# Split weights kept as one tile whose start moves by 8 bytes from use to use

## The chip, the cores and the metric

The kernel runs on one NeuronCore of a Trainium2 chip. The metric is device time in microseconds, from the start of the program on that core to its end. Each time given for a kernel is a median of runs; the profile is one further execution of the same program. The engines are called PE (the matrix engine), DVE (the vector engine), ACT (the scalar engine), POOL and SP; of SP only the queue is used, it issues most of the transfers.

## What is computed

A token block of 256 rows and 1024 columns passes two transformer blocks in float32. The first has two layers, and each layer works on the rows (`lat`) and on a context of 256 rows (`cx`) together; the second has memory attention, dilated attention, a convolution branch and a mixture of 32 experts.

```python
for l in range(DEPTH):                       # first block, two layers
    lat = lat + 0.5 * ml[2] * _swiglu(_modulate(lat, ...), *ffn1)
    cx = cx + 0.5 * mc[2] * _swiglu(_modulate(cx, ...), *ffn1)
    out_lat, _, _ = _token_mixer(_modulate(lat, ...), *mix_w, s_f, s_b)
    lat = lat + ml[5] * out_lat
    lat = lat + 0.5 * ml[8] * _swiglu(_modulate(lat, ...), *ffn2)
...
    proj = h @ w_in[l]                        # second block
    x = x + merged @ w_out[l]
    x = x + _hierarchical_moe(h2, ...)        # 32 experts, top 2 of one group
```

Nearly all of the work is matrix products of float32 activations with float32 weights that are read once.

## The kernel before, in words

**The weight stream.** `plan` lists the weights of both blocks, up to the experts, in the order in which they are used, cut into units of 128 partitions by 2048 floats (1 MB). `Stream.issue` (L295) has SP load a unit into one of three `raw` buffers. `Stream.pump` takes a half of a unit, 1024 floats, and splits it in two: ACT copies it into a tile of the type float32r, which is the high part `wh` (L313), and DVE subtracts that from the original, which is the low part `wl` (L314). There are 428 such halves. They go round in five places, `pst0` to `pst4`, each a pool of its own that holds one `wh` and one `wl`. A place is used again every fifth half, once the matmuls that read it are done. `take` hands out slices of 128 or 512 columns.

**The matmuls.** `mm3` (L402 to L404) forms each product in three passes: low weight by high activation, high weight by low activation, high by high. Weights are the stationary operand, activations (`xh`, `xl`, `hh`, `hl`, in the second block also `om` and `mgh`, `mgl`) move through, 256 or 512 columns at a time. `wide` (L971 to L973) turns the roles round for a few products. The order of all this is the program's own: one stream of instructions per engine, with side work (scan, attention) woven in by a count of estimated time. The matmuls of the scan's masked levels (L855) are ordinary float32 ones; their moving operand is read with a stride, in runs that double in length from level to level.

**The experts.** Their weights are 192 units of 1 MB, loaded whole into whatever buffers come free (`moe_issue`, L1535). In steady state 21 buffers go round: `ring` (7, a tile of its own), `moexh` and `moexl` (2 each, the room of `xh` and `xl`), `X` (1), `moe` (3, the room of `raw`), `moex` (3), `moeom`, `moemgl` and the other `X` (1 each).

**Where the tiles lie.** The pools fill the memory of a partition from both ends. Two tiles are never read or written: `edge`, 8 floats, made ahead of `xh` and `xl`, and `rim`, 56 floats, at the far end beside `raw`. With them `xh`, `xl`, `hh`, `hl`, all ten `wh` and `wl` and the three `raw` start at a multiple of 256 bytes.

Of the kernel before, what the change touches and what calls it, by code (L numbers as in the profile page):

```python
# [9 lines left out]
F = mybir.dt.float32  # L10
R = mybir.dt.float32r
# [9 lines left out]
NRAW, NSPLIT, LOOK, NADA = 3, 5, 2, 8  # L21
# [152 lines left out]
R2_QN, R2_KN, R2_QM, R2_KM, R2_B, NR2 = 0, 64, 128, 256, 384, 420  # L174
SUB = 32
OWN = 7
EDGE = (8, 56)


def level_masks():  # L180
# [96 lines left out]
class Stream:  # L277
# [21 lines left out]
    def pump(self, target):  # L299
        k = self.k  # L300
        while self.hs < target and self.scan < len(self.units):
            kind = self.units[self.scan][0]
            if kind == "d":
                k.mod(*self.units[self.scan][1], self.raw.pop(self.scan))
                self.scan += 1
                self.issue(self.scan + NRAW)
                continue
            if self.hs - self.held >= NSPLIT:
                return
            raw = self.raw[self.scan][:, self.half2 * 1024:self.half2 * 1024 + 1024]  # L310
            p, _ = k.pst[(self.halves - 1 - self.hs) % NSPLIT]
            wh, wl = (p.tile([128, 1024], R, name=n) for n in ("wh", "wl"))
            k.nc.scalar.activation(wh, raw, AF.Copy)  # L313
            k.nc.vector.tensor_sub(wl, raw, wh.bitcast(F))  # L314
            self.sp[self.hs] = (wh, wl)
            self.hs += 1
            self.half2 ^= 1
            if self.half2 == 0:
                self.raw.pop(self.scan)
                self.scan += 1  # L320
                self.issue(self.scan + NRAW)
# [53 lines left out]
class Kernel:  # L375
# [34 lines left out]
    def run(self):  # L410
        tc, nc, a, es = self.tc, self.nc, self.a, self.es
        self.pc = es.enter_context(tc.tile_pool(name="pc", bufs=1))
        self.pw = es.enter_context(tc.tile_pool(name="pw", bufs=1))
        self.prw, _ = self.pool("prw", "right")
        self.pst = [self.pool("pst%d" % i, "right") for i in range(NSPLIT)]
        self.pf, self.pf_end = self.pool("pf", "right")
        self.pm, self.pm_end = self.pool("pm")
        self.ps = es.enter_context(tc.tile_pool(name="ps", bufs=1, space=PSUM))
        pc = self.pc
        self.S = Stream(self, self.units, a["ws"])  # L420
        self.th = Threads()
        self.X = pc.tile([128, 2, 8, 256], F, name="X")
        self.eps = pc.tile([128, 1], F, name="eps")
        self.lbc = pc.tile([128, 2, 2, 4], F, name="lbc")
        self.edge = pc.tile([128, EDGE[0]], F, name="edge")
        self.operands()
        self.cols = pc.tile([128, NCOL], F, name="cols")
        self.cst = pc.tile([128, NCST], F, name="cst")
        load = nc.sync.dma_start
        load(self.cols, a["cols"])  # L430
        load(self.cst, a["cst"])
        self.post = self.pm.tile([128, 512], F, name="post", tag="AB", bufs=4)[:, :256 + 4 * (T // 64)]
        load(self.post, a["post"])
        load(self.X[:, 0], a["xin"][:, 0])
        load(self.X[:, 1], a["xin"][:, 1])
        for u in range(NADA):
            load(self.ada_raw[u], a["ws"][u])
            if u in (1, 3):
                self.S.issue(NADA + (u + 1) // 2)
        self.S.issue(NADA + NRAW)  # L440
        self.msk = self.pm.tile([128, 5, 128], I32, name="msk")
        nc.sync.dma_start(self.msk, a["msk"])
        self.ident = self.cst[:, CST_ID:CST_ID + 128]
        self.ones = self.cst[:, CST_ONE:CST_ONE + 128]
        self.sel = self.cst[:, CST_SEL:CST_SEL + 2]
        nc.gpsimd.memset(self.eps, EPS)
        self.scp = pc.tile([128, 8, 36], F, name="scp", tag="scp")[:, :, 0:32]
        nc.gpsimd.memset(self.scp, 0.0)
        nc.scalar.activation(self.scp[:, :, 0:2], self.col("c", "p (a b) -> p a b", b=2), AF.Silu)
        self.warm()  # L450
        self.lower_bounds()
        self.spread()
        self.mods = [pc.tile([128, 72, 2], F, name=f"mods{l}") for l in range(2)]
        self.stat_tiles()
        self.AB = {}
        self.first()
        self.second()
        self.moe()
# [14 lines left out]


    def operands(self):

        self.ada_tiles()
        self.prw.tile([128, EDGE[1]], F, name="rim")

    def ada_tiles(self):  # L480

# [1374 lines left out]
```

## Time and profile before

| | us |
|---|---|
| median of three runs | 2541.31 (2541.2 to 2541.64) |
| the profiled execution | 2542.87 |
| its span, first to last instruction | 2541.0 |
| PE busy in it | 2389.7 |
| DVE busy | 1398.4 |
| ACT busy | 931.0 |

How to read it: the span is what the trace covers, the execution's own time includes what lies around it. Busy time is an average over stages that have different limits, so it doesn't tell what the end waits for; that is read stage by stage, from the slices, from windows and from the time between one instruction's start and the next one's. A matmul's printed duration is longer than its step, since matmuls overlap.

### The profile page before, as it was taken

To read this page: it belongs to the slowest core of one execution; us is meant where nothing else is said; L and a number is where in the kernel's file an instruction comes from. 1 tells how busy PE (TensorE), PEld (TensorE's weight loads), DVE (VectorE), ACT (ScalarE), POOL (GpSimd) and SP (SyncE) were. 2 spreads that over 40 slices of the span, in tenths; PEclk is the share of its full clock that TensorE was granted. 3 is DMA by queue.
4 is the path that set the end of the run, shared out by engine and by line. 5 is a ranking of instruction groups with operands and counts; after the bars stand their busy time and mean duration, and the time that the engine had idled before them with its cause. 6 is when DMAs were issued, how large, how long until landed. Compare 5 with 4: busy or idle time off the path is not lost.

```text
span 2541.0 us, 34807 instructions
## 1 busy us (share of the span) xinstructions
PE 2389.7 (94%) x14237; PEld 1919.0 (76%) x14237; DVE 1398.4 (55%) x2458; ACT 931.0 (37%) x1479; POOL 92.9 (4%) x125
## 2 busy tenths in 40 slices
PE   8999999999999999999999989999999999767775
PEld 6888888888988888988888879999888993222221
DVE  5777745776787634887534686655776551000000
ACT  5322234666422223422223576545644640000000
POOL 1000001000100001000001000000100000000000
PEclk9999999999999999999999999999999999887877
DMA  7545532112355423455322314455533688999998
GB/s 312 177 176 194 199 116 96 67 51 100 143 222 199 166 100 112 154 205 192 137 97 99 128 68 146 176 182 182 196 147 118 261 319 369 424 424 425 425 424 355
DMA packets 72583, 513.40 MB, mean 202 GB/s; under 512 B 8208, under 2 KB 9760, under 8 KB 10592
## 3 DMA queue, kind: packets, MB, share of 16 engines
q1 hardware_dynamic: 71280, 508.29, 51.9%
q8 instruction: 114, 1.87, 0.3%
q0 software_dynamic: 560, 1.87, 0.2%
q10 hardware_dynamic: 576, 0.94, 0.1%
q14 instruction: 53, 0.43, 0.0%
HBM read 510.01 MB, written 1.05 MB: 201 GB/s over the span
## 4 chain that ended last, share of the span: by engine, by line
PE 44%; DMA 13%; DVE 1%; ACT 1%; issue 0%; POOL 0%; SPq 0%; ACTq 0%; DVEq 0%
PE p L403 5%; PE p L404 5%; PE p L402 5%; DMA ring<-wm 4%; PE po L403 3%; PE po L404 3%; PE po L402 3%; PE pz L402 3%; PE pz L403 3%; PE pz L404 3%; DMA moexh<-wm 2%; DMA moe<-wm 2%; DMA moex<-wm 2%; DMA X<-wm 2%; PE wide L973 1%; PE wide L971 1%
## 5 line engine op out<-in xcount | busy, mean ns | idle before, releaser
L314 DVE TENSOR_TENSOR wl<-raw,wh 128x1024 fp32r<-128x1024 f32 x428 | 525.0, 1228 | 336.3 <-ACT wh L313 333.0
L313 ACT ACTIVATE wh<-raw 128x1024 fp32r<-128x1024 f32 x428 | 451.6, 1057 | 602.2 <-PE po L404 247.7
L402 PE MATMUL p<-xh,wl 128*128 128x512 f32 (+1 forms) x1608 | 554.4, 347 | 1.6 <-ACT xh L613 1.6
L403 PE MATMUL p<-xl,wh 128*128 128x512 f32 (+1 forms) x1608 | 555.0, 346 | 0.1
L404 PE MATMUL p<-xh,wh 128*128 128x512 f32 (+1 forms) x1608 | 554.5, 346 | 0.0
L402 PEld LDWEIGHTS p<-xh,wl 128*128 128x128 f32 x1608 | 303.6, 190 | 41.1 <-ACT xh L613 2.8
L403 PEld LDWEIGHTS p<-xl,wh 128*128 128x128 f32 x1608 | 304.5, 190 | 38.8 <-DVE xl L614 1.1
L404 PEld LDWEIGHTS p<-xh,wh 128*128 128x128 f32 x1608 | 304.6, 190 | 36.9
L513 DVE SCALAR_TENSOR_TENSOR junk<-raw,sc 128x1024 f32<-128x1024 f32 x256 | 302.9, 1227 | 19.6 <-DMA raw<-ws 14.0
L403 PE MATMUL po<-hl,wh 128*128 128x512 f32 (+1 forms) x767 | 266.5, 348 | 0.1
L402 PE MATMUL po<-hh,wl 128*128 128x512 f32 (+1 forms) x767 | 266.4, 348 | 0.0
L404 PE MATMUL po<-hh,wh 128*128 128x512 f32 (+1 forms) x767 | 266.2, 347 | 0.0
L402 PE MATMUL pz<-xh,wl 128*128 128x256 f32 (+1 forms) x672 | 223.8, 333 | 0.0
L403 PE MATMUL pz<-xl,wh 128*128 128x256 f32 (+1 forms) x672 | 212.0, 315 | 0.0
L404 PE MATMUL pz<-xh,wh 128*128 128x256 f32 (+1 forms) x672 | 211.9, 315 | 0.0
L403 PEld LDWEIGHTS po<-hl,wh 128*128 128x128 f32 x767 | 145.2, 189 | 19.0 <-DVE hl L730 0.7
L402 PEld LDWEIGHTS po<-hh,wl 128*128 128x128 f32 x767 | 145.0, 189 | 18.4
L404 PEld LDWEIGHTS po<-hh,wh 128*128 128x128 f32 x767 | 145.2, 189 | 18.1
L727 ACT ACTIVATE ffa<-p 128x512 f32<-128x512 f32 (+1 forms) x88 | 48.0, 545 | 248.7 <-PE p L404 248.7
L402 PEld LDWEIGHTS pz<-xh,wl 128*128 128x128 f32 x672 | 128.4, 191 | 11.6 <-issue 6.2
L404 PEld LDWEIGHTS pz<-xh,wh 128*128 128x128 f32 x672 | 128.3, 191 | 7.5 <-issue 0.2
L403 PEld LDWEIGHTS pz<-xl,wh 128*128 128x128 f32 x672 | 128.7, 191 | 5.7 <-issue 0.5
(423 smaller groups left out, 2887.4 us busy)
## 6 DMA issues: line engine op xcount, KB each, us to landing
raw<-ws SPq DMA_DIRECT2D x279, 1024.0 KB, 4.8
ring<-wm SPq DMA_DIRECT2D x66, 1024.0 KB, 19.8
moe<-wm SPq DMA_DIRECT2D x27, 1024.0 KB, 19.5
moex<-wm SPq DMA_DIRECT2D x27, 1024.0 KB, 19.6
moexh<-wm SPq DMA_DIRECT2D x18, 1024.0 KB, 19.7
moexl<-wm SPq DMA_DIRECT2D x18, 1024.0 KB, 19.6
X<-wm SPq DMA_DIRECT2D x18, 1024.0 KB, 19.7
moeom<-wm SPq DMA_DIRECT2D x9, 1024.0 KB, 19.6
```

The lines of the kernel that those rows point to most:

```text
L313: k.nc.scalar.activation(wh, raw, AF.Copy)
L314: k.nc.vector.tensor_sub(wl, raw, wh.bitcast(F))
L402: mm(out, wl, xh, start=start, stop=False, **kw)
L403: mm(out, wh, xl, start=False, stop=False, **kw)
L404: mm(out, wh, xh, start=False, stop=stop, **kw)
L513: v.scalar_tensor_tensor(junk, raw[:, i * 1024:i * 1024 + 1024], 1.0, self.sc[:, p], op0=OP.mult, op1=OP.mult, accum_out=m[:, t + i, p:p + 1])
L727: nc.scalar.activation(t, p1, AF.Silu)
L971: mm(q[n], self.xl[:, kc, ts], wh, start=kc == 0, stop=False)
L973: mm(q[n], self.xh[:, kc, ts], wh, start=False, stop=kc == 7)
```

## The change

Each place holds one tile `w2` of 2048 floats in place of `wh` and `wl`; these become its two halves. In four of the five places the tile has 16 floats (64 bytes) more, and the pair begins at 0, 2, 4, ... 14 floats into that room, one step further at every use of the place, then at 0 again. The fifth place has no room. `edge` and `rim`, 256 bytes together, are gone, so the sum is the same.

```diff
-EDGE = (8, 56)
+SLIDE = 8
...
             p, _ = k.pst[(self.halves - 1 - self.hs) % NSPLIT]
-            wh, wl = (p.tile([128, 1024], R, name=n) for n in ("wh", "wl"))
+            room = 2 * SLIDE if (self.halves - 1 - self.hs) % NSPLIT else 0
+            at = self.hs // NSPLIT * 2 % room if room else 0
+            w2 = p.tile([128, 2048 + room], R, name="w2")[:, at:at + 2048]
+            wh, wl = w2[:, :1024], w2[:, 1024:]
             k.nc.scalar.activation(wh, raw, AF.Copy)
             k.nc.vector.tensor_sub(wl, raw, wh.bitcast(F))
...
-        self.edge = pc.tile([128, EDGE[0]], F, name="edge")
         self.operands()
...
     def operands(self):
-
         self.ada_tiles()
-        self.prw.tile([128, EDGE[1]], F, name="rim")
```

The built program has the same instructions in the same order on every engine. What differs is the start of the tiles, here as bytes beyond a multiple of 256:

| tile | before | after |
|---|---|---|
| `xh`, `xl`, and in their room `moexh`, `moexl`, two first loads | 0 | 224 |
| `hh`, `hl`, and in their room four first loads | 0 | 224 |
| `raw`, and in its room `moe` | 0 | 224 |
| `wh`, `wl` in the place without room | 0 | 224 |
| `wh`, `wl` in the other four places | 0 | 32, 96, 160 or 224, and 0 to 56 more |
| `ring`, `moex`, `moeom`, `moemgl`, `mgh`, `mgl`, `om` | 96 | 64 |
| `X` | 128 | 128 |

and the count that some waits ask for. These are rows of DVE in the first feed-forward part, before (names with a number are buffers, `PE_49` and the like the semaphores waited for):

```order
L314 TENSOR_TENSOR wl<-raw,wh 128x1024 [waits DMAHW4_49,Activation_49]
L730 TENSOR_TENSOR hl<-ffa,hh 128x512 [waits Activation_49]
L513 SCALAR_TENSOR_TENSOR junk,mods_197<-raw,sc 128x1024 [waits DMAHW0_49]
L314 TENSOR_TENSOR wl<-raw,wh 128x1024 [waits PE_49,Activation_49]
L513 SCALAR_TENSOR_TENSOR junk,mods_197<-raw,sc 128x1024
```

and the same place after:

```order
L317 TENSOR_TENSOR w_850<-raw,w_850 128x1024 [waits DMAHW4_49,Activation_49]
L730 TENSOR_TENSOR hl<-ffa,hh 128x512 [waits Activation_49]
L513 SCALAR_TENSOR_TENSOR junk,mods_195<-raw,sc 128x1024 [waits DMAHW0_49]
L317 TENSOR_TENSOR w_878<-raw,w_878 128x1024 [waits PE_49,Activation_49]
L513 SCALAR_TENSOR_TENSOR junk,mods_195<-raw,sc 128x1024
```

Nothing moved. Where DVE's subtraction waits for PE it asks for a count that is two higher than before (412 in place of 410 at the first such place): the last reader of the whole pair, which ACT's copy ahead of it waits for in both kernels.

## Rows read from the trace of the kernel before

**Rows 1.** The page, section 2: busy tenths of PE and DMA in 40 slices.

```profile
PE   8999999999999999999999989999999999767775
...
DMA  7545532112355423455322314455533688999998
```

**Rows 2.** Windows of core 0: us, busy of each engine, PEclk, DMA share, GB/s.

```profile
800.00:1000.00 200.00, 200.00 (x884) 165.65 (x883) 101.26 (x141) 54.67 (x69) 0.00 (x0) 1.00 0.36 131
2200.00:2300.00 100.00, 69.95 (x524) 25.50 (x520) 6.25 (x14) 5.71 (x12) 0.00 (x0) 0.85 1.01 424
```

**Rows 3.** Timeline of PE, 1262 to 1264 us: start us, us, instruction.

```profile
1261.90 0.39 PE L402 MATMUL po<-hh,wl 128*128 128x512 f32 x1
...
1263.94 0.39 PE L402 MATMUL po<-hh,wl 128*128 128x512 f32 x1
```

**Rows 4.** Timeline of PE, 1650 to 1652 us, at 256 columns.

```profile
1650.02 0.28 PE L402 MATMUL po<-hh,wl 128*128 128x256 f32 x1
...
1652.18 0.28 PE L402 MATMUL po<-hh,wl 128*128 128x256 f32 x1
```

**Rows 5.** Timeline of PE, 2066 to 2068 us, moving operand mgh or mgl.

```profile
2065.87 0.28 PE L402 MATMUL po<-mgh,wl 128*128 128x256 f32 x1
...
2067.67 0.29 PE L402 MATMUL po<-mgh,wl 128*128 128x256 f32 x1
```

**Rows 6.** The page, section 5: busy us, mean ns of one, idle before.

```profile
L314 DVE TENSOR_TENSOR wl<-raw,wh 128x1024 fp32r<-128x1024 f32 x428 | 525.0, 1228 | 336.3 <-ACT wh L313 333.0
```

**Rows 7.** Groups by line and form on VectorE, same columns.

```profile
L622 DVE SCALAR_TENSOR_TENSOR X<-po,Gcol,X 128x256 f32<-128x256 f32 x168 | 75.3, 479 | 87.6 <-PE po L404 87.5
...
L1489 DVE SCALAR_TENSOR_TENSOR cy<-cu,cols,cy 128x256 f32<-128x256 f32 x12 | 5.8, 482 | 0.7 <-DVE cy L1489 0.5
```

**Rows 8.** Timeline of PE, 444 to 460 us, line L855.

```profile
444.47 1.49 PE L855 MATMUL sc<-M,AB 128*128 128x128 f32 x8
...
447.87 1.13 PE L855 MATMUL sc<-M,AB 128*128 128x128 f32 x8
...
457.55 1.06 PE L855 MATMUL sc<-M,AB 128*128 128x128 f32 x8
```

**Rows 9.** The page, section 5: weight loads of one line of three.

```profile
L402 PEld LDWEIGHTS p<-xh,wl 128*128 128x128 f32 x1608 | 303.6, 190 | 41.1 <-ACT xh L613 2.8
...
L402 PEld LDWEIGHTS po<-hh,wl 128*128 128x128 f32 x767 | 145.0, 189 | 18.4
...
L402 PEld LDWEIGHTS pz<-xh,wl 128*128 128x128 f32 x672 | 128.4, 191 | 11.6 <-issue 6.2
```

**Rows 10.** The page, section 6: transfers, KB each, us from issue to landing.

```profile
moe<-wm SPq DMA_DIRECT2D x27, 1024.0 KB, 19.5
...
moexh<-wm SPq DMA_DIRECT2D x18, 1024.0 KB, 19.7
moexl<-wm SPq DMA_DIRECT2D x18, 1024.0 KB, 19.6
```

**Rows 11.** Timeline of SP's queue, 2065 us and 2318 to 2368 us: start us, us.

```profile
2065.38 5.52 SPq L1535 DMA_DIRECT2D moe<-wm  x2
...
2318.07 0.33 SPq L1535 DMA_DIRECT2D moexh<-wm  x1
...
2325.51 0.33 SPq L1535 DMA_DIRECT2D X<-wm  x1
...
2335.39 5.20 SPq L1535 DMA_DIRECT2D moex<-wm  x3
2342.70 0.33 SPq L1535 DMA_DIRECT2D moeom<-wm  x1
2345.16 0.33 SPq L1535 DMA_DIRECT2D moemgl<-wm  x1
...
2350.01 15.20 SPq L1535 DMA_DIRECT2D ring<-wm  x7
2367.36 2.82 SPq L1535 DMA_DIRECT2D moexh<-wm  x2
```

## The prediction

> **What bounds the kernel now.** I read the slices of the page first, then the windows, then single rows of TensorE and of SP's queue. The slices [rows 1] show two stages. Up to about 2050 us PE stands at 9 in nearly every slice and the DMA engines at 1 to 5; after that PE falls to 5 to 7 and DMA stands at 8 or 9. The windows [rows 2] say the same in numbers: from 800 to 1000 us PE is busy 200.00 of 200 us at a granted clock of 1.00 with a DMA share of 0.36; from 2200 to 2300 us PE is busy 69.95 of 100 us while the DMA share is 1.01 at 424 GB/s. So the first four fifths end when TensorE has run its matmuls, and the last 430 us end when the expert weights have arrived. Vector and scalar engine bound nothing: in the first of these windows they are busy 101.26 and 54.67 of 200 us.
>
> How tight the first stage is decides what the change can do there. Matmuls of 512 columns follow each other every 0.2267 us (nine steps in 2.04 us, [rows 3]), those of 256 columns every 0.120 us (eighteen steps in 2.16 us, [rows 4]). At 2.4 GHz the columns alone take 213.3 and 106.7 ns, so each matmul carries the same 13.3 ns on top, whatever its width. The stream has no holes that could be closed; a change of address can only act on a step itself.
>
> **What the change does, part by part.** No engine gets another instruction, and none stands at another place; this is a change of addresses, and of one wait.
>
> *The wait.* A pair is now one tile, so VectorE's write of the low half waits for the last reader of the old pair, two matmuls later than before. ScalarE's write of the high half already waited for that same matmul, and VectorE waits for ScalarE anyway: 333.0 of its 336.3 us of waiting before this line end with ScalarE [rows 6]. Behind it on VectorE stand the dot products of L513 and the residues of L730, and who waits for those is TensorE; but the later of the two waits has not moved. I cost it at nothing; its cover is ScalarE's write of the high half, which always lies between.
>
> *The split's own instructions.* They now write at starts that are 8 bytes apart. Reads 4 and 8 bytes off a round start are in the trace: the convolution's L1489 takes 482 ns, the same form at round starts (L622) 479 [rows 7]. For ScalarE no row has such a write; its bounds are nothing and the 3 ns of VectorE, times 428 writes, 1.3 us of ScalarE's time in a stage where it is busy 54.67 of 200 us [rows 2]. Nothing on the path.
>
> *The moving operands.* The tiles xh, xl, hh and hl move from a multiple of 256 bytes to 224 beyond one. Rows for an operand like that are there: mgh and mgl start 96 bytes beyond, and their 256-column matmuls step at 0.120 us (fifteen in 1.80 us, [rows 5]), as those from hh [rows 4]. Cost: nothing.
>
> *The weights.* This is the part that no row shows, since every split weight starts at a multiple of 256 bytes now. There are 1608 + 767 + 672 loads per line of the three large groups, over three lines 9141 [rows 9]. Four of the five places have room, and of the eight starts four are an odd multiple of 8 bytes: 0.4 of the loads, 3656, begin in the middle of 16 bytes. The nearest rows are the strided reads of L855 [rows 8]. There eight matmuls of 128 columns take 1.06 us where the columns lie in runs of 16, 1.13 us in runs of 2, and 1.49 us where every column lies apart from the one before. So a column that is read alone costs (1.49 - 1.06) / 8 / 128, 0.42 ns; one of a pair (1.13 - 1.06) / 8 / 128, 0.07 ns. A shifted load is still one run, with one broken piece more: between nothing and 0.42 ns if it is read in one stretch. In how many stretches a load is read no row tells; I stop at four, 1.7 ns. Over 3656 loads that is 0, 1.5 or 6.1 us. I take nothing, because runs of pairs, which are far more broken than a run with two odd ends, cost almost nothing; the 6.1 us stay in the range. A gain has no mechanism in the rows but the 13.3 ns, which is a rival below.
>
> The Trainium skill ("SBUF — State Buffer", Specifications) says that SBUF is read in lines of 16 bytes, that a line wants two hits for full bandwidth, and that each crossing to a new line pays. The trace agrees with the first half: pairs are nearly free and single columns are not [rows 8]. By the second half each shifted load pays one crossing more, the sum would be 1.5 us longer, and this is the rule that speaks against the change. [...]
>
> *The transfers.* Here the trace has a price. In the second stage SP keeps eight transfers in flight (19.5 us from issue to landing [rows 10], one every 2.4 to 2.5 us), and each issue follows the landing of the transfer eight places earlier. Buffers come round in the order ring (7), moexh (2), moexl (2), X, moe (3), moex (3), moeom, moemgl, X. So the issues of [rows 11] tell landings: three of ring between 2318.07 and 2325.51, 2.48 us each; one of moexh and two of moexl between 2335.39 and 2342.70, 2.44; two of moe between 2345.16 and 2350.01, 2.43; and the third moe, three moex, moeom, moemgl and X between 2350.01 and 2367.36, 2.48. The fast ones are those that start at a multiple of 256 bytes; ring, moex, moeom and moemgl start 96 beyond one and X 128. Where the tile lies does not sort them: moexh lies low and moe at the top, both are fast. The change takes moexh, moexl and moe to 224 beyond. I price them at 2.48 instead of 2.43, 0.05 us each. There are 27 + 18 + 18 [rows 10]; the first seven (three moe, two of each other) are issued by 2071 us [rows 11], while TensorE still runs the output projection. That leaves 56, and 2.8 us, all of it on the path since the DMA share there is 1.01 [rows 2]. Starts of 64 beyond (ring, moex) and 224 are not in the trace; 96 and 128 cost the same, so I take it that only the multiple of 256 matters. Bounds: nothing, and twice the price, 5.6 us.
>
> In the first 30 us nine loads of 1 MB (adaxh, adaxl, adahh, adahl and raw) lose their round start as well, with the DMA engines at 7 tenths [rows 1]: 0 to 0.45 us, I take 0.4. In between the stream of raw is covered by TensorE, with a DMA share of 0.36 [rows 2]; it would cost if that cover were gone, 0.05 us a unit.
>
> **The sum.** 2.8 + 0.4 = 3.2 us. The profiled execution took 2542.87 us with a span of 2541.0; the median of the three timed runs is 2541.31. I put the difference on the median: 2544.5 us, 0.13% more.
>
> **The rivals.**
> A, the forecast: transfers lose their round start, TensorE notices nothing. 2544.5.
> B, the other side: a load from the middle of 16 bytes is longer by one to four single-column reads, 0.42 to 1.7 ns, on top of A. 2546.0 to 2550.6, at the middle 2548.3. For it: L855's 1.49 us. Against it: L855's 1.13 us, and steps that did not move with mgh. It decides from 0.5 ns a load on. By the Trainium skill's page on SBUF it would be the small end.
> C, the starts are not what sorts the transfers, or the other buffers gain as much at 64 as these lose: the change does nothing that shows. 2541.3. Against it: five tiles sort the same way.
> D, the 13.3 ns that every matmul carries hang on the weights' start and go away on the 3656 loads: 48.6 us less, about 2496. Nothing in the rows speaks for it; they show the 13.3 ns at one start only. E, its mirror, doubles them: about 2593.
>
> **How the numbers follow.** A 0.62, B 0.18, C 0.10, D 0.05, E 0.05. The predicted time is A's. The range takes in A, B and C: from 2541.0 to 2550.6, with 0.1 outside. A measurement of this kernel tells about 0.2%, 5.1 us, from no change, so the border lies at 2546.4: A and C are the same, B crosses it in five sixths of its band. Faster 0.05 (D), slower 0.15 + 0.05 = 0.20, same 0.75.
>
> **What would show it.** Right: in the second stage the fast issues of moexh, moexl and moe stand 2.48 us apart like the rest, and a round of 21 buffers takes 52.1 instead of 51.8 us; the steps of TensorE stay at 0.2267 and 0.120 us on average, though single steps may jitter. B shows as a mean step longer by a nanosecond for four of five halves while the mgh-like shift of the moving side does not matter. C shows as issues that stay at 2.43 us. The prediction is wrong in kind if the end of the first stage (the last matmul of the output projection) moves by more than 1 us; then the price of an address on TensorE was misread.

## The result and the profile after

The changed kernel takes 2560.48 us (2559.06 to 2561.85, three runs), 1.0075 times the time before (95% interval 1.0052 to 1.0098): 19.2 us slower, outside the range that was forecast. The profiled execution took 2561.85 us with a span of 2560.1.

The page's slices tell of the same two stages as [rows 1]:

```profile
PE   8999999999999999999999999999999999776765
...
DMA  7445532112365423454322314555533779999998
```

The windows, same columns as [rows 2], show where the time went: PE is busy all the time at a granted clock of 1.00, as before, but in the same 200 us it starts 868 matmuls where it started 884.

```profile
800.00:1000.00 200.00, 200.00 (x868) 162.88 (x867) 98.64 (x138) 51.89 (x64) 0.00 (x0) 1.00 0.36 132
...
2200.00:2300.00 100.00, 69.09 (x408) 21.27 (x408) 4.73 (x10) 4.73 (x10) 0.00 (x0) 0.74 1.01 421
```

The last matmul of the output projection tells how much the first stage grew. Timeline of PE, before and then after (the next row is the router's):

```profile
2086.74 0.28 PE L404 MATMUL po<-mgh,wh 128*128 128x256 f32 x1
2086.85 0.42 PE L1561 MATMUL lg<-wr,X 128*128 128x36 f32 x3
```

```profile
2101.04 0.29 PE L407 MATMUL po<-mgh,w 128*128 128x256 f32 x1
2101.17 0.31 PE L1561 MATMUL lg<-wr,X 128*128 128x36 f32 x2
```

14.3 us of the 19.1 us by which the span grew lie ahead of this point, 4.8 behind it.

A single step shows what happened. Timeline of PE in the kernel after, one output of the feed-forward part, same columns as [rows 3]. The first rows read weights of the place without room, from 899.84 on those of a place whose pair begins 32 bytes further than `hh` modulo 256:

```profile
898.70 0.39 PE L406 MATMUL po<-hl,w 128*128 128x512 f32 x1
...
899.61 0.40 PE L407 MATMUL po<-hh,w 128*128 128x512 f32 x1
...
900.30 0.40 PE L407 MATMUL po<-hh,w 128*128 128x512 f32 x1
...
902.40 0.40 PE L407 MATMUL po<-hh,w 128*128 128x512 f32 x1
```

Four steps in 0.91 us, 0.2275 each; then nine in 2.10 us, 0.2333 each, where [rows 3] have 0.2267. 0.2267 and 0.2333 us are 544 and 560 cycles of 2.4 GHz: 32 and 48 on top of the 512 columns.

The rows of the three lines of `mm3` stand in the order of the program, so each step can be put beside the two addresses that its matmul reads. I call *distance* the start of the weights less the start of the moving operand, modulo 256. Mean ns from one start to the next, at twelve of the 32 distances that the kernel after has (steps with a stall left out):

```
distance          0      8     16     32     56     64     88    120    168    192    216    224
512, before     226.9  (no other distance)
512, after      227.4  230.7  227.0  233.1  233.2  233.5  233.2  227.2  233.0  229.4  226.7  233.1
256, before     119.8  (om, mgh and mgl at 160: 119.8 to 120.1)
256, after      119.5  116.3  118.4  118.2  117.6  116.7  115.1  119.0  117.0  117.8  119.3  116.9
```

Over all distances 512 columns step at 230.49 ns (226.89 before), 256 columns at 118.46 (119.84), and the 720 matmuls of `wide`, 48 of them of 256 columns, at 223.96 (220.22, their steps to other work among them). So 4899 x 3.60 = 17.6 us lost, 4986 x 1.38 = 6.9 gained, 720 x 3.74 = 2.7 lost: 13.4 of the 14.3 us, stalls left out.

The second stage is the one that was forecast. Timeline of SP's queue, columns as [rows 11]:

```profile
2331.76 2.80 SPq L1535 DMA_DIRECT2D moexh<-wm  x2
...
2341.69 0.33 SPq L1535 DMA_DIRECT2D X<-wm  x1
...
2366.57 5.43 SPq L1535 DMA_DIRECT2D ring<-wm  x3
```

Fourteen issues in 34.81 us, 2.486 each, none of them fast any more. The ten from X to ring take 24.88 us, in [rows 11] 24.50 (2325.51 to 2350.01), and six buffers whose landings were fast (`moexh`, `moexl` and `moe`, two each) land in that stretch: 0.06 us each. A round of 21 buffers, from one `moexh` to the next, takes 51.73 to 51.92 us before and 52.23 to 52.34 after, in four of five rounds each (the fifth takes 53.20 and 53.70).

What answers to the other groups did not move. VectorE still waits for ScalarE [rows 6], a weight load takes what it took [rows 9], transfers in flight take 0.1 to 0.4 us more by the median [rows 10]. From the page, sections 5 and 6:

```profile
L317 DVE TENSOR_TENSOR w<-raw,w 128x1024 fp32r<-128x1024 f32 x428 | 525.2, 1228 | 343.6 <-ACT w L316 339.9
...
L405 PEld LDWEIGHTS p<-xh,w 128*128 128x128 f32 x1608 | 302.3, 189 | 44.6 <-ACT xh L613 3.0
...
moexh<-wm SPq DMA_DIRECT2D x18, 1024.0 KB, 19.8
```

### The profile page after: what moved, and what is told of

Read it like the earlier page. It is cut to its first block, busy times and chain, and to the rows that moved or that the text cites. A ratio compares the mean times of both kernels' runs of the same rounds, so it can differ in the third digit from the quotient of the medians.

```text
span 2560.1 us, 34805 instructions
## 1 busy us (share of the span) xinstructions
PE 2402.0 (94%) x14237; PEld 1912.6 (75%) x14237; DVE 1399.6 (55%) x2458; ACT 931.0 (36%) x1479; POOL 93.9 (4%) x125
## 3 DMA queue, kind: packets, MB, share of 16 engines
q8 instruction: 114, 1.87, 0.3%
q0 software_dynamic: 560, 1.87, 0.2%
## 4 chain that ended last, share of the span: by engine, by line
PE 42%; DMA 14%; DVE 1%; ACT 1%; issue 0%; POOL 0%; SPq 0%; DVEq 0%; ACTq 0%
PE p L405 5%; PE p L406 5%; PE p L407 5%; DMA ring<-wm 5%; PE po L406 3%; PE po L405 3%; PE po L407 3%; PE pz L405 3%; PE pz L406 3%; PE pz L407 3%; DMA moex<-wm 2%; DMA moe<-wm 2%; DMA X<-wm 2%; DMA moexh<-wm 2%; PE wide L971 1%; PE wide L973 1%
## 5 line engine op out<-in xcount | busy, mean ns | idle before, releaser
L317 DVE TENSOR_TENSOR w<-raw,w 128x1024 fp32r<-128x1024 f32 x428 | 525.2, 1228 | 343.6 <-ACT w L316 339.9
L316 ACT ACTIVATE w<-raw 128x1024 fp32r<-128x1024 f32 x428 | 451.9, 1058 | 614.0 <-PE po L407 256.2
L405 PE MATMUL p<-xh,w 128*128 128x512 f32 (+1 forms) x1608 | 557.1, 348 | 1.8 <-ACT xh L613 1.6
L406 PE MATMUL p<-xl,w 128*128 128x512 f32 (+1 forms) x1608 | 557.6, 348 | 0.0
L407 PE MATMUL p<-xh,w 128*128 128x512 f32 (+1 forms) x1608 | 557.2, 347 | 0.0
L405 PEld LDWEIGHTS p<-xh,w 128*128 128x128 f32 x1608 | 302.3, 189 | 44.6 <-ACT xh L613 3.0
L406 PEld LDWEIGHTS p<-xl,w 128*128 128x128 f32 x1608 | 302.9, 189 | 41.7 <-DVE xl L614 1.0
L407 PEld LDWEIGHTS p<-xh,w 128*128 128x128 f32 x1608 | 303.2, 189 | 40.3
L405 PE MATMUL po<-hh,w 128*128 128x512 f32 (+1 forms) x767 | 267.7, 350 | 0.0
L406 PE MATMUL po<-hl,w 128*128 128x512 f32 (+1 forms) x767 | 267.5, 349 | 0.2
L407 PE MATMUL po<-hh,w 128*128 128x512 f32 (+1 forms) x767 | 267.3, 349 | 0.0
L405 PE MATMUL pz<-xh,w 128*128 128x256 f32 (+1 forms) x672 | 223.3, 332 | 0.0
L407 PE MATMUL pz<-xh,w 128*128 128x256 f32 (+1 forms) x672 | 211.0, 314 | 0.0
L407 PEld LDWEIGHTS po<-hh,w 128*128 128x128 f32 x767 | 144.5, 188 | 20.0
L405 PEld LDWEIGHTS po<-hh,w 128*128 128x128 f32 x767 | 144.2, 188 | 19.9
```

Source lines behind the costliest of these rows:

```text
L405: mm(out, wl, xh, start=start, stop=False, **kw)
L406: mm(out, wh, xl, start=False, stop=False, **kw)
L407: mm(out, wh, xh, start=False, stop=stop, **kw)
```

## The experiments

Four theories for the 14 us: (1) the step hangs on the distance; (2) on the weights' own start, in the middle of 16 bytes or not (the rival B of the prediction); (3) on the later wait of the subtraction; (4) on moving operands that start off a multiple of 64. All results first; "first stage" is the start of the last matmul of `mm3`, "rest" the span behind it, the steps are means in ns.

| kernel | us | ratio (95%) | first stage | rest | 512 | 256 |
|---|---|---|---|---|---|---|
| before | 2541.31 | | 2086.7 | 454 | 226.9 | 119.8 |
| after | 2560.48 | 1.0075 (1.0052 to 1.0098) | 2101.0 | 459 | 230.5 | 118.5 |
| e1, no room, no slide | 2545.84 | 1.0015 (1.0006 to 1.0025) | 2085.3 | 457 | 226.9 | 119.8 |
| e2, rim alone | 2562.87 | 1.0084 (1.0068 to 1.0101) | 2103.6 | 456 | 231.4 | 118.6 |
| e3, fixed beginnings | 2553.04 | 1.0046 (1.0029 to 1.0063) | 2093.5 | 458 | 228.7 | 118.9 |
| e5, one tile alone | 2541.97 | 1.0003 (0.9994 to 1.0013) | 2086.2 | 452 | 226.9 | 119.9 |
| e6, slide by 16 | 2560.94 | 1.0078 (1.0061 to 1.0094) | 2101.3 | 458 | 230.7 | 118.6 |
| e7, 168 in the second part | 2545.70 | 1.0017 (1.0007 to 1.0026) | 2088.6 | 455 | 226.9 | 119.6 |
| e8, 88 | 2541.09 | 0.9998 (0.9988 to 1.0008) | 2086.0 | 452 | 227.0 | 119.0 |
| e9, 64 | 2526.01 | 0.9939 (0.9923 to 0.9956) | 2070.2 | 453 | 227.0 | 115.8 |
| e10, 8 | 2546.44 | 1.0025 (1.0015 to 1.0035) | 2088.7 | 455 | 227.0 | 120.0 |

**e1: the starts off a multiple of 256, without the slide.**

```diff
-        self.edge = pc.tile([128, EDGE[0]], F, name="edge")
...
-        self.prw.tile([128, EDGE[1]], F, name="rim")
```

> The kernel before without its two unused tiles: no room, no slide, separate wh and wl. All of xh, xl, hh, hl, wh, wl and raw start 224 bytes beyond a multiple of 256, so weights and moving operands still stand at the same distance (0 modulo 256). Theory 1 (the step of a matmul hangs on the distance between the start of its weights and of its moving operand, modulo 256): steps 0.2267 and 0.120 as before, only the transfers lose, 2543 to 2546 us. Theory 2 (the weights' own start, in the middle of 16 bytes or not, sets it): no weight lies there, the same 2543 to 2546. Theory 3 (the later wait of the subtraction costs the 15 us): gone here, 2543 to 2546. Theory 4 (moving operands that start off a multiple of 64 cost 6 ns per matmul of 512 columns): 4899 x 6.4 ns = 31 us, about 2575.

2545.84 us, with the steps and the first stage of before. Group of PE by form (busy us, mean ns of one; 389 before too):

```profile
L402 PE MATMUL p<-xh,wl 128*128 128x512 f32 x944 | 367.3, 389 | 0.0
```

Theory 4 falls. What is left, 1.0015 of before or 3.8 us (1.5 to 6.4), fits what the transfers lose: four of five rounds of buffers take 52.22 to 52.31 us here, as in the kernel after.

**e2: of the operands of 512 columns only `xh` and `xl` move.** (`om`, `mgh`, `mgl`, `ring` and `moex` lie behind them and go from 96 to 64.)

```diff
-        self.edge = pc.tile([128, EDGE[0]], F, name="edge")
```

> The kernel before without edge alone: weights, hh and hl keep their multiple of 256 bytes, only xh and xl move to 224 beyond one, so their weights stand 32 bytes further than they (distance 32), those of hh and hl 0. Theory 1: the 3504 matmuls of 512 columns from xh and xl step at 0.233 instead of 0.2267 (as the kernel after shows at distance 32), those from hh and hl stay at 0.2267; 256 columns from xh 0.118 instead of 0.120; 22 us more and 6 us less, with 2 us of transfers about 2559. Theories 2 and 3: weights and waits are those of before, about 2543. Theory 4: xh alone, 3504 x 6.4 ns, about 2565.

2562.87 us, as slow as the change itself (the intervals overlap), though every weight starts where it did before. Groups of PE by form (busy us, mean ns of one):

```profile
L402 PE MATMUL p<-xh,wl 128*128 128x512 f32 x944 | 373.4, 396 | 0.0
...
L402 PE MATMUL po<-hh,wl 128*128 128x512 f32 x465 | 181.0, 389 | 0.0
```

The matmuls from `xh` (distance 32) are 7 ns longer, those from `hh` (distance 0, same weights, same places) are not; both are 389 in the kernel before. Steps: 233.3 and 226.8. Neither weights nor waits were touched, so theories 2 and 3 don't explain this loss; e5 and e6 ask whether they add to that of the change. I had said about 2559.

**e3: the slide replaced by five chosen beginnings.**

```diff
+AT = (0, 6, 12, 14, 4)
...
-            at = self.hs // NSPLIT * 2 % room if room else 0
+            at = AT[(self.halves - 1 - self.hs) % NSPLIT]
```

> The kernel after with a fixed beginning in each place instead of the slide: 0, 24, 48, 56 and 16 bytes into the tile in pst0 to pst4, that is distances of 0, 216, 176, 120 and 16 from the moving operand modulo 256, those at which the kernel after steps fastest at 512 columns. Tiles, waits and the other addresses are those of after. Theory 1: mean step at 512 columns (227.4 + 226.7 + 229.8 + 227.2 + 226.8) / 5 = 227.6 ns instead of 230.5, 4899 x 2.9 ns = 14 us back, at 256 columns 119.0 instead of 118.5, 2.5 us lost: about 2549. Theory 2: two of five places begin in the middle of 16 bytes, as many loads as with the slide (0.4): 2560. Theory 3: the wait is that of after: 2560.

2553.04 us: 7.4 us came back, not 11. Four of the five distances stepped as in the kernel after; 216 did not: 231.7 ns here, 226.7 in the kernel after. The same distance, two steps. That was the first sign that the distance doesn't say all.

**e5: the merging and its wait alone.**

```diff
-            wh, wl = (p.tile([128, 1024], R, name=n) for n in ("wh", "wl"))
+            w2 = p.tile([128, 2048], R, name="w2")
+            wh, wl = w2[:, :1024], w2[:, 1024:]
```

> The kernel before, edge and rim kept, with wh and wl as the two halves of one tile without room: of the change only the merging, and with it the later count that the subtraction waits for. Every address is that of before. If distance alone makes the first stage longer: 2541 to 2543. If the later wait costs (theory 3): up to the 15 us of the first stage, 2556.

2541.97 us, no difference. The wait costs nothing, as the prediction had it.

**e6: every weight at a multiple of 16 bytes.**

```diff
-            at = self.hs // NSPLIT * 2 % room if room else 0
+            at = self.hs // NSPLIT * 4 % room if room else 0
```

> The kernel after with a slide of 16 bytes in place of 8 (0, 16, 32, 48 into the room). Every weight now begins at a multiple of 16 bytes. Theory 2 (middle of 16 bytes): the first stage is that of before, about 2545. Theory 1 (distance modulo 256): by the steps that the kernel after and the matmuls alone show at these distances, a mean of 230.7 ns at 512 columns and 118.4 at 256, about 2560, no better than the slide by 8.

2560.94 us, as with 8 bytes. Weights that begin in the middle of 16 bytes are not what makes the change slow.

**e4: matmuls alone, the weights' start moved.** A kernel of its own, with nothing in it but the three passes of `mm3` over eight slices:

```python
for kc in range(8):
    wh, wl = (w2[:, b + dw + kc * 128:b + dw + kc * 128 + 128] for b in (0, 1024))
    xh, xl = (x[:, dm + kc * 512:dm + kc * 512 + N] for x in xs)
    mm(t, wl, xh, start=kc == 0, stop=False)
    mm(t, wh, xl, start=False, stop=False)
    mm(t, wh, xh, start=False, stop=kc == 7)
```

> Matmuls alone: none of the reference's work is done, the output is not its. One pair of float32r weight tiles, one pair of moving tiles, in three passes over eight slices as in the kernel, 48 matmuls for each setting; first the weights' start goes through 0, 8, ... 504 bytes, then the moving operand's through 32, 64, ... 480 with the weights at 0, then both together; at 512 and then at 256 columns; no other engine works. Theory 1: the step at 512 columns is 0.2267 at distances 0, 40, 120 and 216 and 0.233 at 32, 56, 64 to 112, with the moving start giving the mirror image and both together 0.2267 throughout; at 256 columns 0.113 to 0.115 near 88 and 0.120 at 0. Theory 2: it hangs on the weights' start alone, slow at odd multiples of 8, and the moving operand's start does nothing. If the steps are 0.2267 throughout, it takes the other engines' work to slow them (their reads and writes of the same memory).

No other engine works, and at 28 of the 32 distances the steps of 512 columns are within 1 ns of those in the kernel after (not at 16, 24, 40 and 216): at 512 columns 226.7 at 0 and 120, 228 to 234 at all others; at 256 columns 119.7 at 0, 113.5 to 113.8 at 64, 88 and 168, 115.6 to 121.6 else. From 256 bytes on the list repeats within 0.4 ns, so the period is 256. The moving operand's start gives the mirror image at 512 columns within 1 ns; at 256 columns it doesn't everywhere, distance 64 steps at 117.7 or 117.8 that way. With both starts moved together it stays at 227.2 to 227.6 and at 119.8 to 120.0. So it takes no other engine: the step hangs on where TensorE's own two operands start. Missed: 40 and 216 step at 233.3 and 232.0 here, not 226.7, and 16 at 233.4, where the kernel after has 227.0; at 256 columns 64, 88 and 168 are 1.6 to 3.3 ns faster here than there.

**e7 and e8: a better distance for 256 columns.** If the distance decides, the second part of the kernel, nearly all at 256 columns, should have another one than the first. I put `xh` and `xl` into one tile with some room, and from the second mixer on they begin further in (`hh` and `hl` likewise, in the last feed-forward part):

```diff
+    def operand(self, o):
+        self.xh, self.xl = (self.x2[:, o + i * 4096:o + i * 4096 + 4096].rearrange("p (a b) -> p a b", a=8)
+                            for i in range(2))
...
+        if l == 1:
+            self.operand(XSHIFT)
+        return self.norm_cols(l, "m")
```

> The layout without edge and rim (all at distance 0), and from the second mixer's input on the moving operands begin elsewhere in their room: xh and xl 88 bytes further (distance 168, 2832 matmuls of 256 columns), hh and hl in the last feed-forward part 88 bytes earlier (distance 88, 528 matmuls); moexh and moexl begin at a multiple of 256 again. Theory 1: steps of 256 columns fall from 0.1198 to 0.114 (as the matmuls alone show at 168 and 88) or to 0.117 (as the kernel after shows at 168): (2832 + 528) x 3 to 6 ns = 10 to 20 us less than without the shift, 144 matmuls of 512 columns 1 us more; about 2526 to 2536, faster than both kernels. If only the starts before and after mattered and not the distance, 2545.

> The same with distance 88 for xh and xl (168 bytes further) and 64 for hh and hl (64 bytes earlier). Theory 1: 0.1135 (matmuls alone) to 0.1152 (kernel after) per step of 256 columns for 2832 matmuls, 0.114 to 0.117 for 528: 13 to 21 us less than without the shift, about 2524 to 2532. If the distance didn't matter, 2545.

Both wrong: 2545.70 and 2541.09 us, nothing gained at 168 or 88. Timeline of PE in e8, `hh` at distance 64 and then `xh` at 88 (`h` and `x` in the rows):

```profile
1660.02 0.28 PE L402 MATMUL po<-h,wl 128*128 128x256 f32 x1
...
1662.29 0.28 PE L404 MATMUL po<-h,wh 128*128 128x256 f32 x1
```

```profile
1664.20 0.28 PE L402 MATMUL p<-x,wl 128*128 128x256 f32 x1
...
1666.36 0.28 PE L402 MATMUL p<-x,wl 128*128 128x256 f32 x1
```

Twenty steps in 2.27 us, 0.1135, and eighteen in 2.16 us, 0.1200. Over the run `xh` at distance 88 steps at 119.97 ns (2671 matmuls), `hh` at 64 at 113.48 (521); in e7 both, at 168 and 88, stand at 120.

**e9 and e10: the same edit with 64 and with 8.**

> As the two before, with distance 64 for xh and xl (192 bytes further in their room) and for hh and hl (64 bytes earlier) from the second mixer's input on. The kernel with 88 for xh showed 0.120 there, though the matmuls alone had shown 0.1135 at 88; its hh at 64 showed 0.1135 throughout. Theory 1a (the distance says which rhythms of steps are possible, and the way in picks one that then lasts): 0.1135 for hh; for xh 0.1135 or 0.118, by the way in: 2522 to 2536. Theory 1b (the distance alone says it; something else spoils xh at 88): 0.1135 for both, (2832 + 528) x 6.3 ns = 21 us under the flat layout with its slower transfers restored in part, 2522 to 2526.

> The same with distance 8 for xh and xl alone (248 bytes further), hh and hl at 0. Matmuls alone and the kernel after agree at 8 (0.1156 and 0.1163), there is no second rhythm in the records of either. Theory 1a and 1b: 2832 x 3.5 to 4.2 ns = 10 to 12 us less, 144 matmuls of 512 columns 0.6 us more: 2530 to 2535.

e9 takes 2526.01 us, 0.61% less than before (0.44 to 0.77) and the fastest kernel here. Timeline of PE and its last matmul:

```profile
1650.00 0.28 PE L402 MATMUL po<-h,wl 128*128 128x256 f32 x1
...
1652.15 0.28 PE L403 MATMUL po<-h,wh 128*128 128x256 f32 x1
...
2070.23 0.28 PE L404 MATMUL po<-mgh,wh 128*128 128x256 f32 x1
```

Nineteen steps in 2.15 us, 0.1132, where [rows 4] have 0.120; over all 2670 matmuls from `xh` 114.2. The first stage ends 16.5 us earlier than before. Its `ring` and `moex` buffers happen to start at a multiple of 256 as well, and the rest of the span is 4 us shorter than that of e1; in e8 they start there too, and its rest is 452 as well. e10 gained nothing at 8: 120.0 where e4 and the kernel after have 115.6 and 116.3.

**e11: the way in.**

> Matmuls alone again, none of the reference's work, the output is not its. 24 matmuls at one of sixteen other distances (0, 16, ... 240), then 24 at the distance looked at; then the same after VectorE has read the result, so that TensorE stood still first. At 512 columns the distances 0, 16, 40 and 216, at 256 columns 0, 8, 64, 88 and 168. Theory 1a: at 16, 40 and 216 the mean of a group is either 0.2267 or 0.232 to 0.233, by the distance ahead of it; at 64 either 0.1135 or 0.118; at 88 and 168 either 0.1135 or 0.120; at 0 and 8 one value. Theory 1b: one value for each distance, whatever stands ahead.

At 512 columns and distance 16, ahead of it 80 in the first fence and 96 in the second. Timeline of PE:

```profile
366.21 0.39 PE L46 MATMUL q<-xh,w 128*128 128x512 f32 x1
...
368.02 0.39 PE L45 MATMUL q<-xl,w 128*128 128x512 f32 x1
```

```profile
377.30 0.39 PE L46 MATMUL q<-xh,w 128*128 128x512 f32 x1
...
379.17 0.40 PE L45 MATMUL q<-xl,w 128*128 128x512 f32 x1
```

Eight steps in 1.81 us and in 1.87 us, from the same addresses. Coming from 0, 16 or 80 a group at 16 steps at 226.7, from each of the other thirteen at 233.3 to 233.4. At 40 it is 226.7 from two of sixteen and 233 from the rest, at 216 226.7 from three; at 64 and 256 columns 113.3 from twelve and 117.8 from four, at 168 113.3 to 113.9 from eight and 120 from eight. At 0 all sixteen give one value at 256 columns (119.7 to 120.0) and nearly so at 512 (226.6 to 227.8), at 8 and 256 columns 115.5 to 115.7. After a stop of TensorE a group at 16 came out at 233.3 twice and at 226.7 twice. So a distance allows one or more rhythms and the way in picks one, which then lasts. The order of the weights in the other runs bears this out. At 512 columns 16 and 40 always follow 0 in the kernel after and step at 227.0 and 226.8; 40 follows 32 in e4 and steps at 233.3; 216 follows 176 in e3 and 208 in e4, ways that lead to 232.1 here. Two ways e11 doesn't have: 216 follows 152 in the kernel after, 16 follows 8 in e4. The way in doesn't explain e8 and e10: at 88 fifteen of sixteen ways lead to 113.3 to 113.7, at 8 there is only 115.5, and the kernels had 120.

**e12: the moving operand's own start.**

> Matmuls alone, none of the reference's work, the output is not its. This time the moving operand's start goes in steps of 8 bytes, at 256 and at 512 columns, 48 matmuls for each setting: first with the weights at 0, then with the weights at the same start (distance 0), then with distance 64, then with 88 kept. The kernels with 88, 168 and 8 for xh showed 0.120 throughout though matmuls alone show less there; their xh began at 136, 56 and 216 bytes beyond a multiple of 256, each an odd multiple of 8, the moving operands of all other runs at multiples of 32. Theory 5 (a moving operand that starts in the middle of 16 bytes steps at 0.120 whatever the distance): at distance 88 and 64 0.120 at each odd multiple of 8 and 0.1135 to 0.118 at the even ones. If it was the way in alone: no sorting by odd and even, at distance 88 0.1133 in most.

The same distance, 64, with the moving operand at 128 and then at 136 bytes beyond a multiple of 256. Timeline of PE:

```profile
445.50 0.28 PE L52 MATMUL q<-xl,w 128*128 128x256 f32 x1
...
447.54 0.28 PE L52 MATMUL q<-xl,w 128*128 128x256 f32 x1
```

```profile
450.99 0.28 PE L52 MATMUL q<-xl,w 128*128 128x256 f32 x1
...
453.15 0.28 PE L52 MATMUL q<-xl,w 128*128 128x256 f32 x1
```

Eighteen steps in 2.04 and in 2.16 us, 0.1133 and 0.1200. It is so for all starts: with distance 64 kept, the sixteen even multiples of 8 step at 113.3 or 113.5, the sixteen odd ones at 120.0; with 88 kept, multiples of 32 at 113.3, odd multiples of 16 at 118.3, odd multiples of 8 at 120.0 or 120.1. At 512 columns and distance 0, multiples of 32 step at 226.7 to 227.1, odd multiples of 16 but the first at 233.3, odd multiples of 8 at 232.0 to 233.4. So the moving operand's start counts by itself, modulo 32; that of the weights doesn't sort these steps, since with 88 kept the weights lie in the middle of 16 bytes at the fast starts. At 512 columns the order isn't the same at each distance: with 64 and 88 kept, odd multiples of 16 step at 229.0 and 230.0, multiples of 32 at 233.3 to 233.4. In e7, e8 and e10 `xh` began at 56, 136 and 216 bytes, odd multiples of 8; in e9 at 160. I had expected two classes and there are three.

## Why the prediction was wrong

- **What bounds the kernel:** right, though the slices were read roughly: in [rows 1] DMA's 8 begins at 2033 us and PE's digits fall only at 2160. The first stage is PE without holes, so each ns of a step shows: 13.4 of its 14.3 us are steps.
- **The wait, the split's own instructions:** right, nothing (e5; VectorE's write took 1228 ns before and after).
- **The transfers:** right in kind, and by the traces a little small: 0.06 us a transfer instead of 0.05, rounds longer by 0.5 us instead of 0.3. Forecast 2.8 + 0.4 us; e1 has them alone at 3.8 us (1.5 to 6.4). The 0.4 of the first loads no run tells apart. The starts not yet seen, 64 and 224, cost what 96 and 128 cost, as assumed.
- **The moving operands, "cost: nothing":** this is the step that failed first. It rested on `mgh` and `mgl` at 96 bytes, at 0.120 like `hh`. But that row is of 256 columns, and I carried it over to 512 without one; and equal means hid what was to be seen there, since the single steps in the stretch of [rows 5] go from 116 to 125 ns and those of [rows 4] are all 120. It was also bad luck with the row: weights for `mgh` stand at distance 160, one of six of the 32 at which 256 columns step at 119.9 or 120.0 in e4.
- **The weights, "I take nothing":** failed with it. I asked what a start costs by itself, for each operand alone, and looked for the nearest strided rows. At the starts of this change neither has such a price; the pair has. With both moved together to 224 nothing happens (e1), with either moved against the other 512 columns lose 6.6 ns at most distances. L855 [rows 8], from which B got its 0.42 ns, prices a stride of the moving operand, and no start. How many stretches a load is read in no run shows; the four that gave 1.7 ns and the range's 6.1 us have no row, and with all weights at multiples of 16 bytes (e6) the time stayed at 2560.94.
- **The rivals:** B's reason is refuted (e6, e2); its side was right. Its row on a mean step longer by a nanosecond had the sign, not the size, 3.6. D and E came closest in mechanism: the 13.3 ns do hang on addresses. At 512 columns they go to 20 at most distances (half of what E has), at 256 they fall to 6.6 at a few (half of D). I gave the two 0.10 together because no row spoke for them; no row could, since before the change nearly every distance is 0.
- **Its own sign:** "the end of the first stage moves by more than 1 us; then the price of an address on TensorE was misread". It moved by 14.3.

The Trainium skill ("TensorE: Matmul & The Clock Gate", Step-by-step: what each phase is for) calls TensorE's two read ports, one for the streaming operand and one for the weights, independent. In these runs the two operands are not independent in time: the step hangs on the start of the one against the start of the other, 226.8 ns from `hh` and 233.3 from `xh` in e2. Of the line of 16 bytes that the prediction took from the Trainium skill ("SBUF — State Buffer", Specifications) these runs fit one half: a moving operand that begins in the middle of 16 bytes never steps below 119.9 ns at 256 columns (e12), while weights that do may step at 113.3 (distance 88, e11). The 1.5 us that the prediction drew from it for the weights were not to be seen.

That reads of weights for the next matmul and of the moving operand meet in the memory is my account of it; it would fit a step that repeats every 256 bytes, but no row shows a read. Which way in leads to which rhythm I can't say ahead of a run.

## What to carry to other kernels

Where matmuls follow each other without holes and load new weights each time, the starts of both operands are a parameter: look at the step from start to start, not at the duration, and compare it with columns over clock. Here float32r with 512 columns wants distance 0 (modulo 256) and 256 columns 64, with the moving operand at a multiple of 32 bytes; e9 ends its first stage 16.5 us earlier by that. It is no promise: four of sixteen ways in to distance 64 gave 117.8 ns (e11). A row of one width prices an address at that width only, and a price for each operand alone is not one for the pair.

## What the runs showed of the hardware

- A float32r matmul with its own weight load steps at columns plus 16, 32 or 48 cycles of 2.4 GHz in its commonest rhythms: 113.3 and 120.0 ns at 256 columns, 226.7 and 233.3 at 512. Other means lie mostly between, a few above: 121.6 at distance 24 and 234.3 at 96 (e4). Which it is hangs on the distance of the two starts modulo 256, on the moving start modulo 32, and at many distances on what went ahead.
- Rhythms last: in e11 a group settles within some ten matmuls, most at once, and keeps its rhythm to the end of its 24; in e8 `xh` has a mean of 119.97 ns over 2671.
- 1 MB transfers to starts 64, 96, 128 or 224 bytes beyond a multiple of 256 land every 2.48 to 2.49 us, to a multiple of 256 every 2.43 to 2.44.
